# Two merge logit blocks of branch A as a pair of seven products, with filler dealt by need

## The chip, the cores and the metric

One NeuronCore of a Trainium2 chip runs the whole program. The metric is the device time of one execution in microseconds (us). TensorE (PE in the rows) does the matrix products, VectorE (DVE) and ScalarE (ACT) the elementwise work, GpSimd (POOL) some of it, and SyncE (SP) issues nearly all transfers (DMA) as one queue in order.

## What is computed

One encoder layer over 1024 frames and 1024 channels, in float32:

```
h = x @ w_in                     # split into q, k, v, gate_a, alpha_low, pool_in, gate_b, merge_logits
o = gla_chunked(q, k, v, logsigmoid(alpha_low @ w_alpha_up + b_alpha) / 16)    # 4 heads, chunks of 64 frames
y_a = rmsnorm(o) * gla_norm_g * silu(gate_a)                 # branch A, attention
y_b = pool(pool_in) * silu(gate_b)                           # branch B, trailing windows
g_a, g_b = split(sigmoid(merge_logits + b_merge))
y = (g_a * (y_a @ w_proj_a) + g_b * (y_b @ w_proj_b)) @ w_out
out = layernorm(2 ** 0.25 * x + y) * ln_g + ln_b
```

Inside a chunk of the attention every pair of frames (t, s) is weighted by exp(-|G_t - G_s|), in both directions of time; between chunks a state is carried.

## The kernel before, in words

Every float32 product is made of three products of a faster matrix type: each operand is split into a high part, rounded by ACT (`whi`, `xh`), and a rest made by DVE (`wlo`, `xl`), both by `split` at L52 and L53, and high*high, high*low and low*high add up in PSUM.

The program has two stages. The **attention stage** makes q, k and v and runs the four heads one after the other. A head (the loop `for h in range(H)`) builds scaled copies `qs` and `ks` at five distances (`level`), multiplies them (`scores`, into `ps_s`), and DVE merges each result into the tile `Pc` under a mask (L407). `place` copies `Pc` into the block-diagonal tile `P` (L410 on ACT, L411 on DVE). Then `outputs` multiplies `P` with v and `qi` with the carried states `st` (into `ps_o`, L441 and L443). `norm` scales the result, and in the next head `out_t` transposes it (L476) into a staging tile `oTs`, in two halves, whose four DMAs each (L478) store it in DRAM. `ends` prepares the next head: its tiles `e` (L311), `ke` and `cq`, and the decays. A head's own products on PE are small, with long chains on DVE between them, so `fill` puts other products in between, the **filler**: a generator gives one product at a time, with an assumed price (216 ns for 512 columns), and `fill(ns)` takes products until that much is paid. The filler is, in order: the q, k and gate projections of heads 1 to 3 (`q_gen`, `k_gen`, `z_gen`), the rest of v (`v1_gen`, 264 columns each), and the eight blocks of branch A's merge logits (`la_gen`), each 48 products of 512 columns. ACT copies a finished block's logits into the one tile of pool `sg`, and SP stores them (L296). What filler is left when the heads are done runs then.

In the **second stage** every 1024x1024 projection is cut in 2x2 parts and computed with seven part products in place of eight (class `Pair`: two blocks of 128 output channels, 7 x 12 = 84 products of 512 columns, where plain blocks need 2 x 48). The operands are combinations of parts of x (`xT`), y_b, y_a or w_o, made ahead. The pairs run in the order of the list `items`: pool input and its gate (`pi`, `gb`), gate of branch A (`gta`), merge logits of branch B (`lb`), the two projections (`pb`, `pa`), and then the output pairs `o` with the layer norm. `gate_a` loads the stored logits of branch A and applies the sigmoid.

A scheduler decides the order on each engine from the program's order, priorities (`tc.high_priority`) and a simulated timeline. After that every engine runs its own list strictly in that order, and waits where an input, or the buffer it writes, isn't ready. A tag of a pool has `bufs` buffers: tag `E`, with two, holds in turn the level tiles `e`, the tiles of `ends`, and `oTs`.

Of the kernel before, what the change touches and what calls it, by code (L numbers as in the profile page):

```python
# [7 lines left out]
F32 = mybir.dt.float32  # L8
# [3 lines left out]
AF = mybir.ActivationFunctionType  # L12
# [4 lines left out]
P = 128  # L17
S = 1024
D = 1024
KB = D // P  # L20
NT = S // P
H = 4
DV = 256
CH = 64
NPR = S // P
# [11 lines left out]
def encoder_layer(ctx: ExitStack, tc: tile.TileContext, xT, x, w_av, w_v, w_blk, w_up, b_al, g_norm,  # L37
                  w_pool, p_scale, b_mrg, w_pa, w_pb, w_o, ln_g, ln_b, ident_c, rcnt_c, masks_c, out):
    nc = tc.nc
    act, dve, pool_e, pe, sp = nc.scalar, nc.vector, nc.gpsimd, nc.tensor, nc.sync  # L40
# [40 lines left out]
    masks = const.tile([P, 5, CH], U8, name="masks")  # L81
# [4 lines left out]
    bm_t = const.tile([P, 16], F32, name="bm_t")  # L86
# [4 lines left out]
    gla = tc.alloc_tile_pool(name="gla", bufs=1)  # L91
# [51 lines left out]
                        yield n * 0.416 + 3  # L143

    def keep_v(tbs, outs, c0):
        for n, (tb, o) in enumerate(zip(tbs, outs)):
            dst = v[tb][:, c0:c0 + o.shape[1]]
            if n % 2:
                dve.tensor_copy(dst, o)  # L149
            else:  # L150
                act.copy(dst, o)

    accs = [ps_acc.tile([P, S], F32, tag="acc", name=f"ps_v0_{i}") for i in range(2)]
    scs = [ps_sc.tile([P, 512], F32, tag="sc", name=f"ps_v0_{i}") for i in (5, 6)]
# [95 lines left out]
    qt, kt_, gt = {}, {}, {}  # L250

    oT_d = dram.tile([H, 8, 32, 4, NPR, 32], F32, name="oT", tag="oT")
    la_d = [dram.tile([P, S], F32, name=f"la_{j}", tag=f"la_{j}") for j in range(KB)]
    pt = gla.tile([P, NPR, P], F32, name="P")
    pc = gla.tile([P, NPR, CH], F32, name="Pc")
# [5 lines left out]
    def z_gen(h):  # L261

        bias = b_al_t[:, h:h + 1]
        e = gla.tile([P, S], F32, tag="E", name=f"ze_{h}", bufs=2)
        m = gla.tile([P, S], F32, tag="qs", name=f"zm_{h}", bufs=2)
        for half in range(2):
            sl = slice(half * 512, half * 512 + 512)
            ps = ps_m.tile([P, 512], F32, tag="m", name=f"ps_z{h}_{half}")
            pe.matmul(ps, lhsT=up_w[:, h * P:h * P + P], rhs=a_rhs[:, sl], start=True, stop=True)
            act.activation(e[:, sl], ps, AF.Abs, bias=bias)  # L270
            dve.tensor_scalar(out=m[:, sl], in0=ps, scalar1=bias, scalar2=0.0, op0=ALU.add, op1=ALU.min)
            yield 216
        act.activation(e, e, AF.Exp, scale=-1.0)
        act.activation(e, e, AF.Ln, bias=1.0)
        dve.tensor_tensor(out=m, in0=m, in1=e, op=ALU.subtract)
        g = gla.tile([P, S], F32, tag="G", name=f"G_{h}", bufs=2)
        dve.tensor_tensor_scan(out=g, data0=smask, data1=m, initial=0.0, op0=ALU.mult, op1=ALU.add)
        gt[h] = g

    def q_gen(h):  # L280
        def then(ps):
            qt[h] = gla.tile([P, S], F32, tag="q", name=f"q_{h}", bufs=2)
            act.mul(qt[h], ps, QSCALE)
        return w_in_gen(h, f"q{h}", then)

    def k_gen(h):
        def then(ps):
            kt_[h] = gla.tile([P, S], F32, tag="k", name=f"k_{h}", bufs=2)
            dve.tensor_copy(kt_[h], ps)
        return w_in_gen(4 + h, f"k{h}", then)  # L290

    def la_gen(j, pool):
        def then(ps):
            s = pool.tile([P, S], F32, tag="sg", name=f"la_{j}")
            act.copy(s, ps)
            sp.dma_start(la_d[j], s)  # L296
        return w_in_gen(32 + j, f"la{j}", then)
# [97 lines left out]
    def scores(h, hl, li):  # L395

        qs, ks = gs[h][hl]
        ps = ps_sc.tile([P, 512], F32, tag="sc", name=f"ps_s{h}_{hl}")
        psv = ps.rearrange("p (b t) -> p b t", t=CH)
        for b in range(NPR):  # L400
            for c in range(2):
                cs = slice(b * P + c * CH, b * P + c * CH + CH)
                pe.matmul(psv[c * CH:c * CH + CH, b, :], lhsT=ks[:, cs], rhs=qs[:, cs], start=True, stop=True)  # L403
        if hl == 32:
            act.copy(pc, psv)
        else:
            dve.copy_predicated(out=pc, mask=masks[:, li - 1:li, :].to_broadcast([P, NPR, CH]), data=psv)  # L407

    def place(h):
        act.copy(pt[:CH, :, :CH], pc[:CH])  # L410
        dve.tensor_copy(pt[CH:, :, CH:], pc[CH:])  # L411

    def states(h):

        d, hs = gs[h], slice(h * DV, h * DV + DV)
        st = gla.tile([P, NPR - 1, DV], F32, tag="st", name=f"st_{h}", bufs=1)
        d["st"] = st
        for b0 in range(0, NPR - 1, 2):
            ps = (ps_m.tile([P, 512], F32, tag="m", name=f"ps_st{h}_{b0}") if b0 < 4 else
                  ps_sc.tile([P, 512], F32, tag="sc", name=f"ps_st{h}_{b0}"))  # L420
            bs = range(b0, min(b0 + 2, NPR - 1))
            for b in bs:
                pst = ps[:, (b - b0) * DV:(b - b0) * DV + DV]
                pe.matmul(pst, lhsT=d["ket"][:, b, :], rhs=v[b][:, hs], start=True, stop=True)
            with tc.high_priority(offset=100):
                for b in bs:
                    pst = ps[:, (b - b0) * DV:(b - b0) * DV + DV]
                    if b:
                        dve.scalar_tensor_tensor(out=st[:, b, :], in0=st[:, b - 1, :], scalar=d["dec"][:, b:b + 1],
                                                 in1=pst, op0=ALU.mult, op1=ALU.add)  # L430
                    else:
                        dve.tensor_copy(st[:, 0, :], pst)
# [38 lines left out]
    def out_t(h, half):  # L471

        hs = slice(h * DV, h * DV + DV)
        stage = gla.tile([P, 8, 4, 32], F32, tag="E", name=f"oTs_{h}_{half}", bufs=2)
        for b in range(4):
            dve.transpose(stage[:, :, b, :], v[half * 4 + b][:, hs].rearrange("p (j t) -> p j t", t=32))  # L476
        for i in range(4):
            sp.dma_start(oT_d[h, :, :, i, half * 4:half * 4 + 4, :].rearrange("j d b t -> d j (b t)"),  # L478
                         stage[32 * i:32 * i + 32].rearrange("d j b t -> d j (b t)"))


    def v1_gen(grp, tb0):
        acc = [ps_acc.tile([P, S], F32, tag="acc", name=f"ps_v1_{grp}_{tb0 + i}") for i in (0, 2)]
        tbs = range(tb0, tb0 + 4)
        outs = [acc[i // 2][:, i % 2 * 512:i % 2 * 512 + 264] for i in range(4)]
        yield from v_gen(w_v[grp], 264, f"v{grp}_{tb0}", tbs, outs)
        keep_v(tbs, outs, 496 + grp * 264)

    def chain(gens):
        for g in gens:  # L490
            yield from g

    owed = [0.0]

    def fill(ns):
        owed[0] += ns
        while owed[0] > 0:
            t = next(filler, None)
            if t is None:
                return  # L500
            owed[0] -= t

    sg = tc.alloc_tile_pool(name="sg", bufs=1, side="right")
    for g in (q_gen(0), z_gen(0), k_gen(0)):
        for _ in g:
            pass
    filler = chain([q_gen(1), z_gen(1), k_gen(1), v1_gen(0, 0), v1_gen(0, 4),
                    z_gen(2), q_gen(2), k_gen(2), v1_gen(1, 0), v1_gen(1, 4),
                    z_gen(3), q_gen(3), k_gen(3)] + [la_gen(j, sg) for j in range(8)])
    ends(0)  # L510
    starts(0)
    for h in range(H):
        todo = 42500
        steps = 12

        def f():
            fill(todo / steps)

        level(h, 32)
        if h == 0:  # L520
            fill(5000)
            todo -= 5000
        f()
        scores(h, 32, 0)
        cross_chunk(h)
        level(h, 16)
        f()
        k_transposed(h)
        single_frames(h)
        level(h, 8)  # L530
        f()
        scores(h, 16, 1)
        level(h, 4)
        f()
        scores(h, 8, 2)
        states(h)
        level(h, 2)
        if h:
            out_t(h - 1, 0)
        f()  # L540
        scores(h, 4, 3)
        if h:
            out_t(h - 1, 1)
        f()
        scores(h, 2, 4)
        place(h)
        f()
        if h + 1 < H:
            ends(h + 1)
        for b0 in range(0, NPR, 2):  # L550
            f()
            outputs(h, b0)
        if h + 1 < H:
            starts(h + 1)
        norm(h)
        f()
    for g in range(2):
        WO.ahead(g, lambda n, nm: gla.tile([P, 2, 512], F32, tag={"22": "KET", "12": "q", "11": "k", "21": "G"}[n], name=nm,
                                           bufs=1 if n == "22" else 2), dve)
    fill(10400)  # L560
    out_t(H - 1, 0)
    out_t(H - 1, 1)
    fill(1e9)
# [249 lines left out]
    for n, q in enumerate((0, 2, 1, 3)):  # L813
        items.append(gate_pair(f"gta{q}", 8 + 2 * q, AF.Silu, y_a(2 * q), hooks=more[n]))

    def keep(j0):
        def then(t):
            for i in range(2):
                sp.dma_start(gb_d[j0 + i], t(i))
        return then  # L820

    more = [ahead(YA, 0), ahead(YA, 1), None, change(X, YB)]
    for q in range(4):
        items.append(gate_pair(f"lb{q}", 40 + 2 * q, AF.Sigmoid, keep(2 * q), bias=8 + 2 * q, hooks=more[q]))


    m_last = {}
# [32 lines left out]

    def gate_a(t, j, cs):
        sp.dma_start(t, la_d[j][:, cs])
        act.activation(t, t, AF.Sigmoid, bias=bm_t[:, j:j + 1])

    for q in range(4):
        items.append(gated(f"pb{q}", 2 * q, YB, w_pb, lambda t, j, cs: sp.dma_start(t, gb_d[j][:, cs]), None,
# [188 lines left out]
```

## Time and profile before

| | us |
|---|---|
| median of 3 runs (972.33 to 977.69) | 973.58 |
| the profiled execution, its own time | 975.38 |
| its span, first to last instruction | 973.6 |
| PE busy in the span | 932.1 (96%) |
| DVE busy | 750.7 (77%) |
| ACT busy | 399.8 (41%) |
| POOL busy | 111.4 (11%) |

The profiled execution is one run; 1.8 us of its time lie outside its span. Busy shares are averages over both stages. A PE that is busy is not always at its peak, since overlapping products are all counted.

### The profile page before, as it was taken

The page shows a single profiled execution, that of the slowest core. Times are in us where ns is not written, and L with a number is a line of the kernel's source. Part 1 is how long each engine was busy: PE and PEld are TensorE (multiplying, and loading weights), DVE is VectorE, ACT ScalarE, POOL GpSimd, SP SyncE. Part 2 cuts the span into 40 slices and gives each one's busy share as a digit, 9 for nine tenths or more (in the row PEclk, how much of TensorE's full clock was granted, in tenths as well). Part 3 has the DMA queues.
Part 4 walks back from the last instruction along what each step waited for, and adds up shares of the span by engine and source line. Part 5 has one row for each costly group of instructions (what it writes and reads, how often), then busy time and mean ns, then how long its engine had stood idle before and what let it go on. Part 6 is the DMA issues. An engine that isn't in the chain of part 4 may idle for free. (4 is left out here: it accounts for less than half of the span.)

```text
span 973.6 us, 13056 instructions
## 1 busy us (share of the span) xinstructions
PE 932.1 (96%) x4744; PEld 755.8 (78%) x4744; DVE 750.7 (77%) x1144; ACT 399.8 (41%) x676; POOL 111.4 (11%) x59
## 2 busy tenths in 40 slices
PE   9999889899899999999999999999999999997995
PEld 6887887787677787788878788888888888775874
DVE  5459969859859655878696878788788887799787
ACT  5155335235142124433333333345562543544571
POOL 1523313313324000000000000000000000000022
PEclk9999999999999999999999999999999999997998
DMA  9931110330513738243212179799596787679254
GB/s 288 331 109 35 51 53 26 77 103 24 151 49 121 261 127 309 103 154 138 98 54 87 53 258 342 284 343 336 177 344 215 256 307 215 209 233 335 76 109 107
DMA packets 84144, 169.14 MB, mean 174 GB/s; under 512 B 11456, under 2 KB 28096, under 8 KB 84080
## 3 DMA queue, kind: packets, MB, share of 16 engines
q1 hardware_dynamic: 83216, 165.16, 49.7%
q0 software_dynamic: 864, 3.15, 1.9%
q8 instruction: 37, 0.61, 0.3%
q14 instruction: 27, 0.22, 0.1%
HBM read 114.80 MB, written 53.48 MB: 173 GB/s over the span
## 5 line engine op out<-in xcount | busy, mean ns | idle before, releaser
L455 POOL TENSOR_TENSOR rsr_ln<-rsa_ln,mhalf 128x2 f32<-128x2 f32 (+1 forms) x5 | 5.1, 1014 | 583.0 <-PE psc_o L634 571.0
L392 POOL TENSOR_TENSOR ks<-k,e 128x1024 f32<-128x1024 f32 x20 | 57.8, 2900 | 77.3 <-ACT e L388 63.1
L123 PE MATMUL ps_la<-xh,whi_la 128*128 128x512 f32 x128 | 51.3, 401 | 0.0
L123 PE MATMUL ps_la<-xh,wlo_la 128*128 128x512 f32 x128 | 51.1, 399 | 0.0
L123 PE MATMUL ps_la<-xl,whi_la 128*128 128x512 f32 x128 | 51.0, 398 | 0.0
L141 PE MATMUL ps_v<-whi_v,xh 128*128 128x264 f32 x128 | 38.4, 300 | 3.6 <-DVE v L149 3.1
L388 ACT ACTIVATE e<-e 128x1024 f32<-128x1024 f32 x20 | 21.1, 1059 | 42.8 <-DVE e L387 39.6
L141 PE MATMUL ps_v<-whi_v,xl 128*128 128x264 f32 x128 | 38.6, 302 | 0.0
L141 PE MATMUL ps_v<-wlo_v,xh 128*128 128x264 f32 x128 | 38.0, 301 | 0.0
L52 ACT CAST whi_gb<-raw_gb 128x512 fp32r<-128x512 f32 x28 | 17.3, 621 | 49.0 <-PE psd_pi L634 14.8
L391 DVE TENSOR_TENSOR qs<-q,e 128x1024 f32<-128x1024 f32 x20 | 33.5, 1674 | 2.1 <-ACT e L388 2.0
L52 ACT CAST whi_lb<-raw_lb 128x512 fp32r<-128x512 f32 x28 | 17.4, 621 | 37.1 <-PE psd_lb L634 9.3
L52 ACT CAST whi_gta<-raw_gta 128x512 fp32r<-128x512 f32 x28 | 17.3, 618 | 33.9 <-PE psd_gta L634 10.1
L52 ACT CAST whi_pi<-raw_pi 128x512 fp32r<-128x512 f32 x28 | 17.4, 620 | 32.6 <-PE psd_gb L634 7.0
L52 ACT CAST whi_pb<-raw_pb 128x512 fp32r<-128x512 f32 x28 | 17.1, 619 | 32.8 <-PE psd_pb L634 11.2
L446 DVE COPY v<-ps_o 128x256 f32<-128x256 f32 x32 | 13.3, 421 | 21.8 <-PE ps_o L443 15.8
L141 PEld LDWEIGHTS ps_v<-whi_v,xh 128*128 128x128 f32 x128 | 25.3, 198 | 4.5 <-DVE v L149 3.4
L123 PEld LDWEIGHTS ps_la<-xh,whi_la 128*128 128x128 f32 x128 | 24.1, 188 | 5.7 <-issue 0.4
L123 PEld LDWEIGHTS ps_la<-xh,wlo_la 128*128 128x128 f32 x128 | 24.1, 188 | 5.4
L403 PEld LDWEIGHTS ps_s<-qs,ks 128*64 128x64 f32 x640 | 20.8, 138 | 9.5 <-issue 9.3
L123 PEld LDWEIGHTS ps_la<-xl,whi_la 128*128 128x128 f32 x128 | 24.1, 188 | 5.3
L52 ACT CAST whi_o<-raw_o 128x512 fp32r<-128x512 f32 x28 | 16.9, 617 | 25.1 <-DVE raw_o L619 8.8
(586 smaller groups left out, 3066.4 us busy)
## 6 DMA issues: line engine op xcount, KB each, us to landing
raw_v<-in_w_v SPq DMA_DIRECT2D x16, 264.0 KB, 2.6
xp<-in_xT SPq DMA_DIRECT2D x8, 512.0 KB, 6.8
oT<-oTs SPq DMA_DIRECT2D x32, 128.0 KB, 2.6
raw_la<-in_w_blk SPq DMA_DIRECT2D x8, 512.0 KB, 3.5
wop<-in_w_o SPq DMA_DIRECT2D x8, 512.0 KB, 4.3
la<-la SPq DMA_DIRECT2D x8, 512.0 KB, 3.6
raw_pi<-in_w_blk SPq DMA_DIRECT2D x16, 256.0 KB, 3.8
raw_gb<-in_w_blk SPq DMA_DIRECT2D x16, 256.0 KB, 2.6
```

What stands on the lines that cost most here:

```text
L52: act.copy(hi, src)
L123: pe.matmul(ps[:, half * 512:half * 512 + 512], lhsT=a, rhs=mov(b, k, half), start=(i == 0), stop=(i == 23))
L141: pe.matmul(o, lhsT=sta(a, k, tb), rhs=w(k - k0)[b], start=(k == 0 and i == 0), stop=(k == KB - 1 and i == 2))
L388: act.activation(e, e, AF.Exp, scale=1.0 / TAU)
L391: dve.tensor_tensor(out=qs, in0=qt[h], in1=e, op=ALU.mult)
L392: pool_e.tensor_tensor(out=ks, in0=kt_[h], in1=e, op=ALU.mult)
L403: pe.matmul(psv[c * CH:c * CH + CH, b, :], lhsT=ks[:, cs], rhs=qs[:, cs], start=True, stop=True)
L446: dve.tensor_copy(v[b][:, hs], po)
L455: pool_e.tensor_tensor(out=r, in0=a, in1=mhalf[:, :w], op=ALU.pow)
```

## The change

It does six things. (1) `NLA = 6`: only six of branch A's eight logit blocks stay in the filler; blocks 6 and 7 become a `gate_pair` named `la6`, which stands in `items` between the last `gta` and the first `lb`, and stores finished gates, so that `gate_a` leaves out the sigmoid for them. (2) `todo`, the filler dealt per head, goes from 42500 to 38500 ns, and the portion ahead of the last head's transposes from 10400 to 18000. (3) `until` takes filler until a named point of it is passed: head h's v before `states(h)`, the next head's k before `ends(h + 1)`. (4) The copies in `keep_v`, `scores` and `place` get a priority raised by 100. (5) `out_t` stages heads 0 to 2 in the one tile of pool `sg` and no longer in tag `E`; the last head stays in `E`. (6) `keep` takes the tensor it stores to.

```diff
@@ keep_v, the copies of scores, and place
+        with tc.high_priority(offset=100):
@@ out_t
-        stage = gla.tile([P, 8, 4, 32], F32, tag="E", name=f"oTs_{h}_{half}", bufs=2)
+        pool, tag = (sg, "sg") if h < H - 1 else (gla, "E")
+        stage = pool.tile([P, 8, 4, 32], F32, tag=tag, name=f"oTs_{h}_{half}", bufs=1 if h < H - 1 else 2)
@@ filler
+    passed = set()
+    def mark(nm):
+        passed.add(nm)
+        yield 0
+    def until(nm):
+        while nm not in passed:
+            owed[0] -= next(filler)
...
-    filler = chain([q_gen(1), z_gen(1), k_gen(1), v1_gen(0, 0), v1_gen(0, 4),
-                    z_gen(2), q_gen(2), k_gen(2), v1_gen(1, 0), v1_gen(1, 4),
-                    z_gen(3), q_gen(3), k_gen(3)] + [la_gen(j, sg) for j in range(8)])
+    filler = chain([q_gen(1), z_gen(1), k_gen(1), mark("k1"), v1_gen(0, 0), v1_gen(0, 4), mark("v1"),
+                    z_gen(2), q_gen(2), k_gen(2), mark("k2"), v1_gen(1, 0), v1_gen(1, 4), mark("v2"),
+                    z_gen(3), q_gen(3), k_gen(3), mark("k3")] + [la_gen(j, sg) for j in range(NLA)])
...
-        todo = 42500
+        todo = 38500
...
+        if 0 < h < 3:
+            until(f"v{h}")
         states(h)
...
         if h + 1 < H:
+            until(f"k{h + 1}")
             ends(h + 1)
...
-    fill(10400)
+    fill(18000)
     out_t(H - 1, 0)
@@ second stage
+    for j in range(NLA, KB, 2):
+        items.append(gate_pair(f"la{j}", 32 + j, AF.Sigmoid, keep(la_d, j), bias=j,
+                               hooks=ahead(WO, (j - NLA) // 2) if NLA < 6 else None))
...
     def gate_a(t, j, cs):
         sp.dma_start(t, la_d[j][:, cs])
-        act.activation(t, t, AF.Sigmoid, bias=bm_t[:, j:j + 1])
+        if j < NLA:
+            act.activation(t, t, AF.Sigmoid, bias=bm_t[:, j:j + 1])
```

Lines of the changed kernel are a few numbers higher than before. The orders below name a tile with its buffer number, and the line first.

The first place is DVE's list in head 2, from the merge of the second-last scores (`ps_s_4`) to the half of `place` that DVE does. Before:

```order
L407 COPY_PREDICATED Pc<-masks,ps_s_4_2269 128x512
L322 TENSOR_TENSOR cq_2371<-q_2173,e_3_2362 128x512
L325 TENSOR_TENSOR cq_2371<-q_2173,k_2335 128x8x32 x2
L327 TENSOR_TENSOR cq_2371<-q_2173,e_3_2368 128x16
L329 TENSOR_TENSOR cq_2371<-q_2173,k_2335 128x16
L407 COPY_PREDICATED Pc<-masks,ps_s_2_2313 128x512
L328 TENSOR_TENSOR cq_2371<-cq_2371,k_2335 128x16
L330 TENSOR_TENSOR cq_2371<-q_2173,ke_2372 128x16
L386 TENSOR_TENSOR e_32_2535<-G_2022 128x16x32
L387 TENSOR_TENSOR e_32_2535<-G_2022 128x16x32
L411 COPY P<-Pc 64x8x64
```

And the same stretch of DVE's list in the changed kernel:

```order
L410 COPY_PREDICATED Pc<-masks,ps_s_4_2212 128x512
L324 TENSOR_TENSOR cq_2346<-q_2274,e_3_2337 128x512
L329 TENSOR_TENSOR cq_2346<-q_2274,e_3_2343 128x16
L410 COPY_PREDICATED Pc<-masks,ps_s_2_2254 128x512
L415 COPY P<-Pc 64x8x64
```

The next head's products with k and its first level tile `e_32`, which stood ahead of the copy into `P`, stand behind it now. In heads 0 and 1 they stay ahead of it.

The second place is DVE's list in head 1, with the transposes of head 0's outputs (`oTs_0` and `oTs_1`, the two halves) and the tile `e` of `ends`. Before:

```order
L476 STREAM_TRANSPOSE oTs_1_1624<-v_107 128x8x32
L429 SCALAR_TENSOR_TENSOR st_1554<-st_1554,dec_1082,ps_st_4_1565 128x256
L307 COPY egl_1718<-e_2_1716 128x16
L53 TENSOR_TENSOR wlo_v_0_4_0_1756<-raw_v_0_4_1753,whi_v_0_4_0_1755 128x528
L309 TENSOR_TENSOR dec_1720<-egl_1718 128x8
L429 SCALAR_TENSOR_TENSOR st_1554<-st_1554,dec_1082,ps_st_6_1570 128x256
L289 COPY k_1670<-ps_k_1520 128x1024
L53 TENSOR_TENSOR wlo_v_0_6_0_1795<-raw_v_0_6_1792,whi_v_0_6_0_1794 128x528
L311 TENSOR_TENSOR e_2_1722<-G_1357 128x1024
L407 COPY_PREDICATED Pc<-masks,ps_s_4_1606 128x512
```

And in the changed kernel, from the last transpose of the first half to the first of the second:

```order
L481 STREAM_TRANSPOSE oTs_0_1543<-v_103 128x8x32
L53 TENSOR_TENSOR wlo_v_0_2_0_1735<-raw_v_0_2_1732,whi_v_0_2_0_1734 128x528
L436 COPY st_1516<-ps_st_0_1517 128x256
L313 TENSOR_TENSOR e_2_1678<-G_1394 128x1024
L311 TENSOR_TENSOR dec_1676<-egl_1674 128x8
L433 SCALAR_TENSOR_TENSOR st_1516<-st_1516,dec_1055,ps_st_0_1517 128x256
L433 SCALAR_TENSOR_TENSOR st_1516<-st_1516,dec_1055,ps_st_2_1522 128x256 x2
L481 STREAM_TRANSPOSE oTs_1_1598<-v_104 128x8x32
```

The tile `e` of `ends` is written between the two halves' transposes now and no longer behind both; five other instructions stand between the halves as well.

The third place is SP's list in head 3: the stores of head 2's two halves (`oTs_0` and `oTs_1`), the loads `wop` of w_o, and the stores of logit blocks, whose tile in `sg` the changed kernel shares with `oTs`. Before:

```order
L296 DMA la_518<-la_2669 128x1024
L216 DMA wop_1_3082<-in_w_o 128x2x512
L478 DMA oT<-oTs_0_2772 32x8x128 x4
L216 DMA wop_1_3078<-in_w_o 128x2x512
L216 DMA wop_1_3080<-in_w_o 128x2x512
L478 DMA oT<-oTs_1_2815 32x8x128 x4
L216 DMA wop_0_3056<-in_w_o 128x2x512
```

And in the changed kernel:

```order
L298 DMA la_517<-la_2633 128x1024
L217 DMA wop_1_2976<-in_w_o 128x2x512
L217 DMA wop_1_2978<-in_w_o 128x2x512
L483 DMA oT<-oTs_0_2696 32x8x128 x4
L217 DMA wop_0_2954<-in_w_o 128x2x512
L483 DMA oT<-oTs_1_2738 32x8x128 x4
```

Two loads into the buffers of tags `q` and `k`, which stood between the two halves' stores, stand ahead of both now.

## Rows read from the trace of the kernel before

**Rows 1.** The page: busy us, share of the span and instructions of each engine.

```profile
PE 932.1 (96%) x4744; PEld 755.8 (78%) x4744; DVE 750.7 (77%) x1144; ACT 399.8 (41%) x676; POOL 111.4 (11%) x59
```

**Rows 2.** Stretches: from:to, length, busy us by engine, granted clock, DMA.

```profile
85.00:129.00 44.00, 38.30 (x354) 33.05 (x353) 40.46 (x55) 21.36 (x29) 15.10 (x6) 0.95 0.18 55
129.00:196.00 67.00, 61.94 (x484) 53.37 (x483) 54.16 (x85) 25.53 (x46) 18.90 (x7) 0.98 0.18 47
196.00:270.00 74.00, 68.96 (x499) 57.81 (x500) 56.93 (x98) 29.04 (x52) 19.29 (x7) 0.98 0.30 92
...
640.00:740.00 100.00, 100.00 (x433) 81.04 (x432) 80.90 (x109) 51.65 (x74) 0.00 (x0) 1.00 0.83 300
```

**Rows 3.** Who PE waited for from 60 to 340 us: total us, times, longest.

```profile
PE ps_o L441 <- ACT P L410: 4.0, 1, 4.0
PE ps_o L441 <- DVE P L411: 3.4, 2, 2.7
PE ps_v L141 <- DVE v L149: 3.1, 1, 3.1
PE ps_s L403 <- DVE egl L307: 2.6, 2, 1.3
PE ps_st L424 <- DVE Pc L407: 2.2, 2, 1.6
PE ps_v L141 <- DVE k L289: 0.5, 1, 0.5
PE ps_s L403 <- DVE Pc L364: 0.5, 1, 0.5
```

**Rows 4.** PE in order of time: filler, first outputs of heads, first pair.

```profile
132.61 0.28 PE L141 MATMUL ps_v<-whi_v,xl 128*128 128x264 f32 x1
132.73 1.02 PE L441 MATMUL ps_o<-v,P 128*128 128x256 f32 x4
...
196.25 2.08 PE L441 MATMUL ps_o<-v,P 128*128 128x256 f32 x4 [4.02 <-ACT P L410]
...
269.67 1.10 PE L441 MATMUL ps_o<-v,P 128*128 128x256 f32 x4 [2.71 <-DVE P L411]
...
333.40 1.10 PE L441 MATMUL ps_o<-v,P 128*128 128x256 f32 x4 [0.69 <-DVE P L411]
...
375.79 0.39 PE L634 MATMUL psa_pi<-xh,whi_pi 128*128 128x512 f32 x1
```

**Rows 5.** DVE in order of time, heads 0 to 2: start, us, idle before.

```profile
128.53 0.42 DVE L411 COPY P<-Pc 64x512 f32<-64x512 f32 x1
...
189.54 1.23 DVE L311 TENSOR_TENSOR e<-G 128x1024 f32<-128x1024 f32 x1 [3.48 <-DMA oT<-oTs]
...
260.42 1.23 DVE L311 TENSOR_TENSOR e<-G 128x1024 f32<-128x1024 f32 x1 [2.72 <-DMA oT<-oTs]
261.57 1.22 DVE L289 COPY k<-ps_k 128x1024 f32<-128x1024 f32 x1
...
268.39 0.68 DVE L387 TENSOR_TENSOR e<-G 128x512 f32<-128x512 f32 x1
```

**Rows 6.** The stores of oTs: issue ns (min/median/max), and time to landing.

```profile
L478 SPq DMA_DIRECT2D oT<-oTs x32: 302/463/1479, 177.4 to 365.0; - x32
...
DMA to landing us min/median/max: 2.1/2.6/4.7
```

**Rows 7.** ACT at the seam: the first pair's first weight.

```profile
370.35 0.62 ACT L52 CAST whi_pi<-raw_pi 128x512 fp32r<-128x512 f32 x1 [4.49 <-DMA raw_pi<-in_w_blk]
```

**Rows 8.** SP's queue at the seam.

```profile
377.32 0.33 SPq L296 DMA_DIRECT2D la<-la  x1
377.69 0.43 SPq L209 DMA_DIRECT2D xT<-xT_0d  x1
```

**Rows 9.** DVE: the eight multiplies of norm, in head 1 and head 3.

```profile
150.91 5.40 DVE L469 SCALAR_TENSOR_TENSOR v<-v,rsr_o,gn 128x256 f32<-128x256 f32 x8
...
355.99 3.26 DVE L469 SCALAR_TENSOR_TENSOR v<-v,rsr_o,gn 128x256 f32<-128x256 f32 x8
```

More of the change, by code (lines that the diff above doesn't have):

```diff
@@ L145, in keep_v @@
     def keep_v(tbs, outs, c0):
[L146 to L151, printed above, removed]
+        with tc.high_priority(offset=100):
+            for n, (tb, o) in enumerate(zip(tbs, outs)):
+                dst = v[tb][:, c0:c0 + o.shape[1]]
+                if n % 2:
+                    dve.tensor_copy(dst, o)
+                else:
+                    act.copy(dst, o)
     accs = [ps_acc.tile([P, S], F32, tag="acc", name=f"ps_v0_{i}") for i in range(2)]
@@ L252, in encoder_layer @@
     oT_d = dram.tile([H, 8, 32, 4, NPR, 32], F32, name="oT", tag="oT")
+    NLA = 6
     la_d = [dram.tile([P, S], F32, name=f"la_{j}", tag=f"la_{j}") for j in range(KB)]
@@ L403, in scores @@
                 pe.matmul(psv[c * CH:c * CH + CH, b, :], lhsT=ks[:, cs], rhs=qs[:, cs], start=True, stop=True)
[L404 to L407, printed above, removed]
+        with tc.high_priority(offset=100):
+            if hl == 32:
+                act.copy(pc, psv)
+            else:
+                dve.copy_predicated(out=pc, mask=masks[:, li - 1:li, :].to_broadcast([P, NPR, CH]), data=psv)
     def place(h):
-        act.copy(pt[:CH, :, :CH], pc[:CH])
-        dve.tensor_copy(pt[CH:, :, CH:], pc[CH:])
+        with tc.high_priority(offset=100):
+            act.copy(pt[:CH, :, :CH], pc[:CH])
+            dve.tensor_copy(pt[CH:, :, CH:], pc[CH:])
     def states(h):
@@ L814, in encoder_layer, with keep @@
         items.append(gate_pair(f"gta{q}", 8 + 2 * q, AF.Silu, y_a(2 * q), hooks=more[n]))
-    def keep(j0):
+    def keep(d, j0):
         def then(t):
             for i in range(2):
-                sp.dma_start(gb_d[j0 + i], t(i))
+                sp.dma_start(d[j0 + i], t(i))
         return then
+    for j in range(NLA, KB, 2):
+        items.append(gate_pair(f"la{j}", 32 + j, AF.Sigmoid, keep(la_d, j), bias=j,
+                               hooks=ahead(WO, (j - NLA) // 2) if NLA < 6 else None))
     more = [ahead(YA, 0), ahead(YA, 1), None, change(X, YB)]
     for q in range(4):
-        items.append(gate_pair(f"lb{q}", 40 + 2 * q, AF.Sigmoid, keep(2 * q), bias=8 + 2 * q, hooks=more[q]))
+        items.append(gate_pair(f"lb{q}", 40 + 2 * q, AF.Sigmoid, keep(gb_d, 2 * q), bias=8 + 2 * q, hooks=more[q]))
     m_last = {}
```

## The prediction

> **What bounds the kernel now.** I read the page first. PE is busy 96% of the span, DVE 77% [rows 1], so the question is where PE loses time and whether DVE stands behind it. The view by stretches gives both. In the second stage (640 to 740 us) PE is busy all the time with 433 products in 100 us, that is 0.231 us for a product of 512 columns; DVE is busy 81% [rows 2]. Each product put there or taken away counts in full. In the attention stage DVE is busy 40.5 of the 44 us of head 0 and 54.2 and 56.9 us of the 67 and 74 us that follow [rows 2]. There PE waits: the view of PE's waits adds up to 16.3 us, for DVE or for what DVE releases, and the largest (4.0 and 3.4) are first products with `P` that wait for `place` [rows 3]. The granted clock of these three stretches is 0.95, 0.98 and 0.98 [rows 2], which is 2.2, 1.3 and 1.5 us of full clock lost: stretches at the lower of TensorE's two levels (1.2 GHz, against 2.4) behind the waits.
>
> PE's list in order of time shows the heads: the first output product starts at 132.73, 196.25, 269.67 and 333.40 us, and the first pair at 375.79 [rows 4]. The intervals are 63.5, 73.4, 63.7 and 42.4 us, and PE waits in the first three for 5.3 (4.0 and 1.3), 4.6 (2.7, 1.3 and 0.6) and 0.7 us, in head 0 for the other 5.7 [rows 3, 4].
>
> Two causes can be read from DVE's list. In heads 1 and 2 the tile `e` at L311 stood 3.48 and 2.72 us at the head of DVE's queue until a store of `oTs` had read its buffer of tag `E`, and the merges of the scores and `place` stood behind it [rows 5]. And in head 2 the order puts k's copy (1.22 us), the products with k and `e_32` (two of 0.68) ahead of the copy into `P` [rows 5].
>
> **The arithmetic.** Two logit blocks fewer are 2 x 48 = 96 products, 96 x 0.231 = 22.2 us; a pair more is 84 products, 19.4 us. Net 2.8 us off. The pair's conversions (7 high parts on ACT, 7 rests and 10 sums on DVE) lie beside PE in a stage where DVE has 19 us in 100 free [rows 2]; if that cover failed, PE would wait for DVE there, which it does nowhere between 640 and 740.
>
> The Trainium skill ("TensorE: Matmul & The Clock Gate", section "Wait — 56ns, not 53.3ns?") gives 215.7 ns from one product of 512 columns to the next at full clock. The rows show 231, 7% more, at a clock of 1.00; by the page's figure the two numbers would be 20.7 and 18.1 us, net 2.6, and nothing else in the sum would change.
>
> **The waits, head by head.** What an interval takes is the longer of PE's own work and DVE's. From the order I counted the filler in each interval. A product of v's 264 columns takes 0.12 us [rows 4].
>
> *Up to head 0's first output.* DVE works nearly without a gap, and its list up to the copy into `P` holds the same work as before. That copy ended at 128.95 [rows 5], but PE came only at 132.73, because it had waited itself (for v's PSUM buffer, which `keep_v` frees late, and for merges) and had run at the lower clock. With these copies raised PE comes in time: first output at 129, DVE's bound. In that time it does 28 v products more and one of 512 columns less, 3.2 us. Bounds: 126 (DVE's few gaps go) to 132.7 (as now).
>
> *Head 0 to head 1.* Filler: the same 96 products of 512 columns, 100 v products in place of 131, so 3.8 us less. PE's own work is 63.5 - 5.3 - 3.8 = 54.4 us. DVE has 54.2 us of work [rows 2], plus the next head's `e_32` (1.4 us), which comes ahead of `P` now, plus waits that stay: some 2 us at PE's pace during the outputs, and a new one. The staging tile has one buffer now, so the second half's transposes wait for the first half's four stores: 4 x 0.46 us of issue and 2.6 of landing [rows 6], 4.5 us, of which `e`, written between the halves now, covers 1.2 [rows 5], and six short instructions some more: a wait of 0.5 to 3.3. I take 2. Behind those transposes at DVE's head stand the merges and `place`, and PE waits for these. Sum 59.6 us: DVE sets this interval, PE idles 5 us in it as before, and the first output starts at 188.6. Bounds 55 to 64.
>
> *Head 1 to head 2.* 102 products in place of 132, and 134 v products for 131: 6.6 us less. PE's own: 73.4 - 4.6 - 6.6 = 62.2, with 1.5 us of clock loss left in. DVE: 56.9 less `e_32` done earlier and what goes behind `P` (1.22 + 1.4 + small ones), about 52, and 4 of waits. PE sets it; with 1.3 us for waits that no order excludes, 63.5: next first output at 252.1. Bounds 60.7 (no wait, no clock loss) to 67.
>
> *Head 2 to head 3.* 166 products for 193: 6.2 us less. 63.7 - 0.7 - 6.2 = 56.8, and 1.5 us for the shared tile, since the logit stores use it too: 58.3, next at 310.4. Bounds 56.8 to 62.
>
> *Head 3 to the first pair.* 116 products for 155: 9.0 us less, 42.4 - 9.0 = 33.4. The cover shrinks: 84 products (19.4 us) follow the last output product in place of 107 (24.7), 5.3 us less. The first pair's first weight is converted at 370.35 to 370.97 [rows 7], 4.8 us ahead of need, and its loads follow the last head's outputs, so it comes 0.5 us late; the next weights perhaps another 0.5. The loads of `xT` stand in SP's queue right behind the last logit store [rows 8], before and after, so they shift with the end of the filler and cost nothing new. I take 1 us: first pair at 344.8. Bounds 0 to 5.3, all of the lost cover.
>
> Before, the first pair came at 375.8, so 31.0 us are gained; the added pair takes 19.4: net 11.6. That is 2.8 of arithmetic and 8.8 of the 21.3 us that waits and clock cost, with the seam's 1 us taken off. The sigmoids that `gate_a` leaves out, the marks of `until` and the rest of the second stage I cost at nothing: the list of the output pairs, where the kernel ends, is nearly unchanged. The profiled execution took 975.4; 975.4 - 11.6 = 963.8. The median of the runs is 1.8 below that execution, so I predict **962**.
>
> **The rivals.** *All waits go.* If DVE keeps pace between heads 0 and 1 too (54.4 in place of 59.6) and the small allowances (1.3, 1.5, 1.0 and 1.5 of clock) vanish, 10.5 more: 951.5. For it: DVE's waits for stores are gone from tag `E`. Against it: 54.2 us of DVE work alone already fills that interval.
>
> *The waits change places.* Less filler means that PE reaches each dependency sooner, and DVE's work does not shrink. If DVE, at 52 us of work with gaps like today's 13 (67 less 54.2), sets the interval after head 1 as well, that costs some 3 us, the interval after head 2 another 2 or 3, and the seam 3: about 971. The Trainium skill ("Perfetto Trace Analysis", section "Optimizing Scalar/DVE Operations") speaks for it: GpSimd and DVE share a port for reading SBUF. The trace agrees so far: the eight multiplies of `norm` took 5.40 us in head 1, and 3.26 in head 3 [rows 9]; GpSimd worked 18.9 us in the first of these stretches [rows 2]. In a shorter interval GpSimd's work lies denser.
>
> *Slower, through the single staging tile.* In head 3 the first half's stores stand in SP's list behind two loads of w_o that need buffers of `q` and `k`, free only when the last level is built; the second half's transposes stand at DVE's head ahead of both last merges and `place`. In head 1 they also do. If the transposes wait 7 to 8 us there and not 0.5 to 3.3, in each of three heads, 16.5 us are lost against the forecast and the kernel passes 978.5. For it speaks that a store in tag `E` already held DVE 3.48 us [rows 5]; against it that in head 2 eleven other instructions stand between the halves.
>
> **Chances.** Forecast, 957 to 968.7: 0.53. All waits gone, below 957: 0.17. Changed places, 968.7 to 978.5: 0.21. Slower, above: 0.09. A measurement of this kernel tells about 0.5% from no change, 4.9 us either way of 973.6. So: faster 0.70, same 0.21, slower 0.09. The range is 953 to 974: it reaches into the first two rivals and leaves out the slow one.
>
> **What would show it.** First output products at about 129, 189, 252 and 310, and the first pair at 345 us. No wait of L313 for a store of `oTs`, but one of the transposes, up to 3.3 us, in heads 1 and 3. PE's largest wait is that for `P` in head 1, about 5 us; in head 2 hardly any. The pair `la6` takes 19 to 20 us. Wrong would make it: a wait of more than 5 us at the transposes, a second long wait for `P`, or a seam where PE waits for the first weights or `xT` by more than 3 us.

## The result, and the profile after

The changed kernel takes 969.14 us (median of 13 runs, 966.51 to 971.98) against 975.12 for the kernel before, run with it (13 runs); the ratio is 0.9931, 95% interval [0.9913, 0.995], that is 4.9 to 8.5 us less. Forecast were 962 us and 11.6 us less. The sign and the range held; the size is about half, and the profiles show that it came about in another way than forecast.

The page of the changed kernel, busy us by engine (it answers to [rows 1]): PE is busy 6.6 us less, and DVE 14 us more in a shorter span.

```profile
PE 925.5 (96%) x4732; PEld 753.1 (78%) x4732; DVE 765.0 (79%) x1156; ACT 400.7 (42%) x680; POOL 110.0 (11%) x59
```

PE's list in order of time, the first output product of each head, the first pair, and the first products of the pair `la6` and of the one after it (answers to [rows 4]):

```profile
129.94 0.59 PE L445 MATMUL ps_o<-v,P 128*128 128x256 f32 x2
...
190.79 0.45 PE L445 MATMUL ps_o<-v,P 128*128 128x256 f32 x1 [0.72 <-DVE P L415]
...
255.42 0.38 PE L445 MATMUL ps_o<-v,P 128*128 128x256 f32 x1
...
316.10 0.48 PE L445 MATMUL ps_o<-v,P 128*128 128x256 f32 x1
...
354.61 0.50 PE L651 MATMUL psa_pi<-xh,whi_pi 128*128 128x512 f32 x1
...
611.19 0.40 PE L651 MATMUL psa_la<-xh,whi_la 128*128 128x512 f32 x1
...
630.52 0.39 PE L651 MATMUL psa_lb<-xh,whi_lb 128*128 128x512 f32 x1
```

The first pair comes 21.2 us earlier (forecast 31.0), and `la6` takes 19.33 us (forecast 19.4). From the first pair to the end of the span it was 973.6 - 375.8 = 597.8 us and is 965.4 - 354.6 = 610.8: 13.0 us more and not 19.4. So two errors of opposite sign stand in the sum. The stretches between those starts (columns as in [rows 2]):

```profile
85.00:129.94 44.94, 41.88 (x402) 37.03 (x402) 41.55 (x56) 21.40 (x29) 12.14 (x6) 1.00 0.20 61
129.94:190.79 60.85, 55.91 (x433) 47.25 (x431) 55.95 (x88) 25.95 (x47) 20.67 (x7) 0.97 0.18 47
190.79:255.42 64.63, 61.67 (x470) 52.80 (x471) 54.35 (x86) 27.70 (x50) 16.30 (x6) 0.97 0.32 97
255.42:316.10 60.68, 57.30 (x399) 45.74 (x397) 50.01 (x79) 17.81 (x35) 18.44 (x7) 1.00 0.35 114
316.10:354.61 38.51, 35.33 (x146) 28.42 (x146) 16.74 (x37) 7.52 (x22) 1.64 (x1) 0.96 0.55 178
```

And who PE waited for from 60 to 360 us (answers to [rows 3]):

```profile
PE ps_st L428 <- DVE Pc L410: 6.0, 4, 2.1
PE ps_o L445 <- ACT ps_o L451: 5.1, 3, 3.1
PE ps_q L123 <- DVE v L150: 1.9, 1, 1.9
PE ps_s L405 <- DVE st L433: 1.4, 1, 1.4
PE ps_s L405 <- DVE qs L393: 1.2, 1, 1.2
PE ps_s L405 <- DVE Pc L366: 1.1, 1, 1.1
PE ps_o L445 <- DVE P L415: 0.7, 1, 0.7
```

These add up to 17.4 us, where 16.3 stood before [rows 3], and the granted clock of the five stretches costs 1.8 + 1.9 + 1.5, about 5.3 us, where it was 5.0. The 7.4 us of waits for `P` have become 0.7, and others have come: 6.0 for the merges of the scores and 5.1 for the outputs' PSUM buffers. In sum nothing of waits and clock was recovered; the 21.2 us are about the price of the 96 products of the two blocks, 22.2.

The largest single wait, 3.1 us, stands in head 3. DVE's list there:

```profile
320.38 5.07 DVE L198 TENSOR_TENSOR wop<-wop,wop 128x1024 f32<-128x1024 f32 x4 [3.80 <-DMA wop<-in_w_o]
325.38 0.42 DVE L450 COPY v<-ps_o 128x256 f32<-128x256 f32 x1
326.37 0.76 DVE L450 COPY v<-ps_o 128x256 f32<-128x256 f32 x2 [0.57 <-ACT ps_o L451]
327.76 0.42 DVE L450 COPY v<-ps_o 128x256 f32<-128x256 f32 x1 [0.64 <-ACT ps_o L451]
```

and PE's, a few us later:

```profile
327.39 1.22 PE L445 MATMUL ps_o<-v,P 128*128 128x256 f32 x2 [3.12 <-ACT ps_o L451]
```

The four sums of w_o's second group (L198) stood at DVE's head for 3.80 us, until a load had landed, and worked for 5.07 us. The copies of the outputs (L450) stood behind them; the squares on ACT wait for the copies, and PE's third output for the squares. The load was that of a tile in `KET`, which the first group must have left:

```profile
314.45 0.38 SPq L217 DMA_DIRECT2D wop<-in_w_o  x1
```

The two products after the wait took 1.22 us, about twice the 0.59 of the first output row above, and the granted clock is 0.96 in this stretch and 0.50 from 327 to 329 us: the wait brought a piece at the lower of the two levels with it.

### The profile page after: what moved, and what is told of

It is laid out like the page before. It is cut to its first block, busy times and chain, and to the rows that moved or that the text cites. A ratio compares the mean times of both kernels' runs of the same rounds, so it can differ in the third digit from the quotient of the medians.

```text
span 965.4 us, 13072 instructions
## 1 busy us (share of the span) xinstructions
PE 925.5 (96%) x4732; PEld 753.1 (78%) x4732; DVE 765.0 (79%) x1156; ACT 400.7 (42%) x680; POOL 110.0 (11%) x59
## 5 line engine op out<-in xcount | busy, mean ns | idle before, releaser
L394 POOL TENSOR_TENSOR ks<-k,e 128x1024 f32<-128x1024 f32 x20 | 55.4, 2771 | 96.5 <-ACT e L390 47.0
L390 ACT ACTIVATE e<-e 128x1024 f32<-128x1024 f32 x20 | 21.2, 1059 | 57.2 <-DVE e L389 57.2
L123 PE MATMUL ps_la<-xl,whi_la 128*128 128x512 f32 x96 | 38.8, 404 | 0.0
L123 PE MATMUL ps_la<-xh,whi_la 128*128 128x512 f32 x96 | 38.3, 399 | 0.0
L123 PE MATMUL ps_la<-xh,wlo_la 128*128 128x512 f32 x96 | 38.3, 399 | 0.0
L52 ACT CAST whi_pi<-raw_pi 128x512 fp32r<-128x512 f32 x28 | 17.4, 620 | 37.7 <-DMA raw_pi<-in_w_blk 9.5
L393 DVE TENSOR_TENSOR qs<-q,e 128x1024 f32<-128x1024 f32 x20 | 30.9, 1543 | 2.3 <-ACT e L390 1.6
L52 ACT CAST whi_lb<-raw_lb 128x512 fp32r<-128x512 f32 x28 | 17.4, 621 | 36.6 <-PE psd_lb L651 8.5
L123 PE MATMUL ps_q<-xh,whi_q 128*128 128x512 f32 x64 | 25.8, 404 | 2.0 <-DVE v L150 1.9
L53 DVE TENSOR_TENSOR wlo_pi<-raw_pi,whi_pi 128x512 fp32r<-128x512 f32 x28 | 19.2, 686 | 10.5 <-ACT whi_pi L52 10.5
L405 PE MATMUL ps_s<-qs,ks 128*64 128x64 f32 x640 | 23.6, 225 | 3.7 <-DVE st L433 1.4
L123 PE MATMUL ps_k<-xh,whi_k 128*128 128x512 f32 x64 | 26.6, 416 | 0.0
L123 PE MATMUL ps_k<-xh,wlo_k 128*128 128x512 f32 x64 | 26.2, 409 | 0.0
```

Source lines behind the costliest of these rows:

```text
L52: act.copy(hi, src)
L53: (lo_eng or dve).tensor_tensor(out=lo, in0=src, in1=hi.bitcast(F32), op=ALU.subtract)
L123: pe.matmul(ps[:, half * 512:half * 512 + 512], lhsT=a, rhs=mov(b, k, half), start=(i == 0), stop=(i == 23))
L390: act.activation(e, e, AF.Exp, scale=1.0 / TAU)
L393: dve.tensor_tensor(out=qs, in0=qt[h], in1=e, op=ALU.mult)
L394: pool_e.tensor_tensor(out=ks, in0=kt_[h], in1=e, op=ALU.mult)
```

## The experiments

Times are medians, ratios are to the kernel before on the same chip. "The changed kernel" is 969.14 us, 0.9931.

| run | edit | us | ratio, 95% interval |
|---|---|---|---|
| e1 | all edits but the pair | 977.25 | 1.0012 [0.9994, 1.003] |
| e2 | the pair alone | 990.94 | 1.0141 [1.0121, 1.0161] |
| e3 | second group's sums on GpSimd | 964.62 | 0.9873 [0.9857, 0.989] |
| e4 | staging back in tag E | 968.5 | 0.9906 [0.9887, 0.9925] |
| e5 | output copies on ScalarE | 957.23 | 0.9803 [0.9783, 0.9822] |
| e6 | no raised copies | 967.88 | 0.9917 [0.9896, 0.9937] |
| e7 | old filler numbers | 983.9 | 1.0078 [1.0058, 1.0099] |
| e8 | e3 and e4 | 966.42 | 0.9892 [0.9872, 0.9912] |
| e9 | fixed turn of weight buffers, as in the changed kernel | 980.75 | 1.005 [1.003, 1.007] |
| e10 | fixed turn, as in the kernel before | 982.25 | 1.0073 [1.0049, 1.0096] |
| e11 | e3 and e5 | 957.9 | 0.9815 [0.979, 0.9839] |
| e12 | the kernel before, output copies on ScalarE | 976.53 | 1.0008 [0.9988, 1.0028] |

The theory after the result: **the gain in the attention is the products taken away; the waits only changed places.** The rival is the forecast's own: the dealing, the raised copies and the staging recover waits by themselves.

**e1, the dealing without the pair**

```diff
-    NLA = 6
+    NLA = 8
```

> All eight logit blocks stay in the filler and no pair is added; every other edit of the change is kept. If the gain of the change is arithmetic and the waits only change places (my theory), this is the kernel before within its noise: 972 to 977 us, PE waits between 60 us and the first pair still 14 to 18 us. If the dealing by need, the raised copies and the staging recover waits of their own, as the forecast had it (8.8 us), it is 964 to 968 us with waits under 10.

No difference to before. Its waits from 60 us to the first pair add up to 20.8 us, more than my 14 to 18, and the first pair comes at 376.39 (before 375.79). With the new numbers, the dealing, the raised copies and the staging together recover nothing; at these numbers the rival falls (e7 shows another side of it).

**e2, the pair without the dealing**

```diff
 (kernel before)
-    ... [la_gen(j, sg) for j in range(8)])
+    ... [la_gen(j, sg) for j in range(6)])
+    for j in range(6, KB, 2):
+        items.append(gate_pair(f"la{j}", 32 + j, AF.Sigmoid, keep(la_d, j), bias=j, ...))
```

> The kernel before with blocks 6 and 7 moved into a pair and nothing else changed (42500 ns of filler per head, 10400 at the end, no raised copies, staging in tag E). My theory: the filler is dealt out too early, so that few products stand between the last output and the first pair; PE then waits 10 to 18 us for the first weights, and the kernel takes 983 to 992 us; the change's other edits are what makes the pair pay. Rival, the move of the blocks alone brings the gain and the other edits nothing: 967 to 971 us.

As expected: 13.9 us slower than before. PE's waits from 60 to 370 us, the first three rows:

```profile
PE psa_pi L635 <- ACT whi_pi L52: 15.0, 1, 15.0
PE ps_o L442 <- ACT P L411: 4.0, 1, 4.0
PE ps_o L442 <- DVE P L412: 3.4, 2, 2.7
```

The order up to head 3 is that of before, so the missing 96 products are missing at the end, where they covered the last head's norm, its transposes, its stores and the first loads of weights.

**e3, the sums of w_o's second group on GpSimd**

```diff
-    WO.ahead(g, ..., dve)
+    WO.ahead(g, ..., (dve, pool_e)[g])
```

> The changed kernel with the four sums of w_o's second group on GpSimd in place of DVE. In the changed kernel these four stand at DVE's head in head 3, wait 3.8 us for a load and hold the copies of the outputs, and PE waits 3.1 us for those at half the clock afterwards. My theory: that wait goes, the interval from head 3's first output to the first pair shrinks from 38.5 to 34 to 35 us, 964 to 966 us in all. Rival, the end of the attention hangs on the chain of norm, stores and first loads anyway: the first pair comes as late as now, 968 to 970 us.

The last stretch of this kernel, from head 3's first output to the first pair:

```profile
315.01:348.42 33.41, 33.41 (x147) 27.59 (x147) 13.06 (x33) 7.77 (x21) 11.86 (x5) 1.00 0.62 204
```

38.51 has become 33.41, PE is busy for all of it, and the clock is 1.00. The theory holds: 5.1 us of this stretch hung on those sums. GpSimd took 10.45 us for the four, where DVE takes 5.07, and nothing waited for it. Of the 5.1 us, PE's wait is 3.1; most of the rest goes with the clock. e10 (below) has the same sums on DVE and the same wait (3.2 us), but a clock of 1.00, and its last stretch takes 36.89:

```profile
314.38:351.27 36.89, 33.70 (x147) 27.41 (x147) 16.72 (x37) 7.51 (x21) 1.64 (x1) 1.00 0.54 180
```


**e4, the staging of the transposes back in tag E**

```diff
-        pool, tag = (sg, "sg") if h < H - 1 else (gla, "E")
-        stage = pool.tile(..., tag=tag, bufs=1 if h < H - 1 else 2)
+        stage = gla.tile(..., tag="E", bufs=2)
```

> The changed kernel with the transposes of heads 0 to 2 staged in the two buffers of tag E again, everything else kept. If the separate staging is worth what the forecast gave it (waits of 3.5 and 2.7 us of e for a store gone from DVE's head, 2 given back at the transposes): 972 to 975 us. If the waits only change places (my theory): within 1.5 us of the changed kernel, 968 to 971 us, with e waiting for stores again and the transposes and the logit copy no longer.

The waits for the stores of `oTs` in this kernel, from 60 to 352 us; L313 writes the tile `e` of `ends` that DVE makes, L306 the other one, which ACT makes:

```profile
DVE oTs L480 <- DMA oT<-oTs: 1.4, 1, 1.4
DVE e L313 <- DMA oT<-oTs: 0.6, 2, 0.3
ACT e L306 <- DMA oT<-oTs: 17.4, 2, 12.6
```

On DVE the waits of `e` [rows 5] do not come back with the old staging (0.6 us). They come back on ACT, whose `e` takes over the buffers that the stores hold; before and in the changed kernel ACT's list shows no wait for these stores at this tile. So it is not the separate tile that freed DVE's head. The pair is not it either, since in e2 DVE's `e` still waits 6.2 us. Of the numbers, `until` and the raised copies no run shows which does it. With the separate tile the transposes wait 4.0 us (two waits, the longest 2.7), and ACT's copy of a logit block 3.6 us for a store. The intervals of the two ratios overlap, so the separate staging is worth nothing that can be told.

**e5, the output copies on ScalarE**

```diff
-            dve.tensor_copy(v[b][:, hs], po)
+            act.copy(v[b][:, hs], po)
```

> The changed kernel with the copies of the output blocks (32 of 0.42 us) on ScalarE in place of DVE. My theory: DVE's work sets the interval from head 0's to head 1's first output (60.8 us in three kernels, whatever PE did in it), so with 3.4 us less of it that interval shrinks to 57 to 58.5; and the sums of w_o at DVE's head in head 3 hold no copy any more, so the last interval is 34 to 35: 960 to 963 us. Rival, not DVE's amount of work but the chain of the merges sets the first interval (or ScalarE delays its own exponentials): it stays at 60 to 61, and only the last interval shrinks: 964 to 966 us.

The best of the twelve: 1.97% below before. Its stretches:

```profile
85.00:130.06 45.06, 41.96 (x403) 37.11 (x401) 41.66 (x56) 21.40 (x29) 12.28 (x6) 1.00 0.20 61
130.06:190.00 59.94, 55.93 (x429) 46.79 (x427) 52.78 (x80) 28.35 (x55) 17.83 (x7) 0.97 0.19 48
190.00:252.82 62.82, 61.94 (x482) 53.39 (x481) 51.65 (x79) 30.45 (x58) 17.75 (x7) 1.00 0.33 100
252.82:308.28 55.46, 55.46 (x394) 45.08 (x392) 42.89 (x69) 20.83 (x43) 17.17 (x7) 1.00 0.36 117
308.28:341.59 33.31, 33.31 (x148) 27.45 (x146) 14.06 (x29) 10.69 (x30) 1.64 (x1) 1.00 0.67 220
```

The total is below what I expected, but the gain does not stand where I expected it. Between heads 0 and 1 DVE has 3.2 us less work and the interval shrinks by 0.9 only: the amount of DVE's work does not set that interval, and this part of my theory fell. PE still waits 4.0 us there, 2.7 of it in one wait for a merge. The gain stands in the interval after head 2 (60.68 to 55.46) and in the last (38.51 to 33.31); in both PE no longer waits at all. Of the 5.2 us after head 2, some 1.4 are six filler products that lie in the interval before it now.

**e6, without the raised copies** (the three `with tc.high_priority(offset=100):` of the change left out)

> The changed kernel without the three raised priorities (the copies into v, of the scores and into P). Few instructions change their place (one copy of v's, two merges on DVE, some ten products on PE). My theory: no difference, 967 to 971 us, first output of head 0 within 1 us of 129.9. If the forecast's reason for that first output (the raised copies bring PE there in time) holds, it comes at 131.5 to 133 and the kernel takes 971 to 973.

No difference that can be told, and head 0's first output comes at 129.72. The forecast's reason for it, the raised copies, falls. What comes with the early output is shown under e7 and e12.

**e7, the old numbers**

```diff
-        todo = 38500
+        todo = 42500
...
-    fill(18000)
+    fill(10400)
```

> The changed kernel with the numbers of before: 42500 ns of filler per head and 10400 ahead of the last transposes. My theory: the numbers are what keeps products for the end of the attention; with the old ones PE waits 10 to 15 us for the first weights of the second stage, 980 to 988 us. Rival, the heads wait less with more filler in each and the end has cover enough: 967 to 972 us.

PE's waits from 60 to 365 us, the first three:

```profile
PE psa_pi L651 <- ACT whi_pi L52: 15.7, 1, 15.7
PE ps_st L428 <- DVE Pc L410: 4.2, 4, 1.8
PE ps_v L141 <- DVE v L150: 3.2, 1, 3.2
```

The wait for the first weights, 15.7 us where I expected 10 to 15, is the one of e2. But e7 is faster than e2, 1.0078 against 1.0141, some 6 us, and both have the pair and the old numbers: here the other edits (`until`, the raised copies, the staging) do recover waits. PE's waits other than that for the weights add up to 11.2 us, and to 16.2 in e2, and those for `P`, 7.4 us in e2, are 1.1. With the new numbers this gain is gone (e1). No run has these edits with the old numbers and without the pair, so what they are worth alone stays open.

Head 0's first output comes at 132.88, as before, with the copies raised; in the ten kernels with 38500 it comes at 129.6 to 130.9, raised or not. The stretch up to it:

```profile
85.00:132.88 47.88, 41.95 (x377) 36.75 (x376) 44.71 (x57) 22.02 (x29) 17.65 (x7) 0.93 0.19 57
```

The clock is 0.93 in it, as before and in e2, and 1.00 in all ten kernels with 38500. e12 shows that the share of filler is not needed for that.

**e8, e3 and e4 together**

> The second group's sums of w_o on GpSimd and the staging back in tag E, the rest as changed. The first alone gave 964.6, the second alone 968.5 against about 969. If the two work in different places (last interval; heads 1 to 3), they add up: 962 to 964 us, last interval 33.5 to 34.5. If tag E gained only because it let the sums of w_o come earlier, it adds nothing: 964 to 966 us.

They do not add up. The last interval is 34.2 us, and the 966.42 lie just above the second reading. That tag E gained by letting the sums come earlier fits e4's own last interval (34.79, against 38.51), and is not shown beyond that.

**e9 and e10, the turn of the weight buffers**

The high and low parts of each split weight go into four buffers each. In the compiled programs these are taken in another turn (order) in the second stage of the kernel before than in the changed one. Both experiments fix the turn:

```diff
 (changed kernel)
-        hi = ring.tile(..., tag="whi")
-        lo = ring.tile(..., tag="wlo")
+        k = turn[0] % 4; turn[0] += 1
+        hi = ring.tile(..., tag=f"whi{W[k]}", bufs=1)
+        lo = ring.tile(..., tag=f"wlo{L[k]}", bufs=1)
 e9:  W = 1,3,0,2   L = 2,3,0,1
 e10: W = 3,2,1,0   L = 2,3,1,0
```

> The changed kernel with the four buffers each of the split weights (high and low part) taken in a fixed turn, the turn that the changed kernel's second stage has. From 550 us on, a product started every 0.2303 us in the changed kernel and five of its variants, and every 0.2320 us in the kernel before and three others, at a granted clock of 1.00 in all ten. My theory: where the parts of the weights lie decides it; here 0.2303 again. The total depends on the attention too, whose turn is also fixed now: 965 to 975 us. Rival, the places do not matter: the pace is the same here and in the next run, whichever it is.

> As the run above, each engine's instructions in the same order, with the turn of the slower four kernels: the high parts in the other order of buffers, the low parts with two of four exchanged. Theory: 0.2320 us per product from 550 us on, and 2.5 to 3 us more than the run above in all (1700 products by 0.0017). Rival: no difference above 1 us.

Busy time and products of PE in the same 100 us of the second stage, first in the kernel before:

```profile
650.00:750.00 100.00, 100.00 (x433) 81.04 (x432) 78.91 (x109) 49.44 (x72) 0.00 (x0) 1.00 0.80 284
```

in the changed kernel:

```profile
650.00:750.00 100.00, 100.00 (x436) 81.61 (x435) 80.37 (x113) 48.65 (x72) 0.00 (x0) 1.00 0.77 269
```

in e9:

```profile
650.00:750.00 100.00, 100.00 (x436) 81.61 (x435) 77.66 (x106) 50.05 (x73) 0.00 (x0) 1.00 0.80 283
```

and in e10:

```profile
650.00:750.00 100.00, 100.00 (x433) 81.02 (x432) 77.39 (x107) 49.81 (x74) 0.00 (x0) 1.00 0.81 278
```

436 products with the one turn and 433 with the other, the same instructions in the same order, at a granted clock of 1.00: the place of the weights' parts decides the pace, and it followed the turn in the two new kernels as it had in the ten profiles before. Whether the turn of the high parts or that of the low parts does it, these two runs can't tell, since both change. The four `lb` pairs show it too: from first to last start of their 336 products 77.70 us before, 77.14 changed, 77.14 in e9 and 77.71 in e10. The total follows less clearly: 1.5 us between the medians, with intervals that overlap, where I expected 2.5 to 3. Both miss the 965 to 975 us that I expected of e9: by their ratios they are some 12 and 14 us slower than the changed kernel. The loss stands in the second stage, which takes 625.8 us in e9 and 610.8 in the changed kernel; PE's waits there add up to 18.0 us in e9, where they were 10.5, and the largest new ones are for the tiles `gb` (5.9).

**e11, e3 and e5 together**

> The output copies on ScalarE and the second group's sums of w_o on GpSimd, the rest as changed. The copies alone gave 957.2 and left no wait behind head 2's outputs. If the sums held nothing but those copies: 955.5 to 958.5, no gain. If taking 5 us more from DVE in head 3 still helps, or GpSimd slows DVE: outside of that, to either side.

No gain over e5: the sums held nothing but those copies.

**e12, the kernel before with the output copies on ScalarE**

> The kernel before with one edit, the copies of the output blocks on ScalarE in place of DVE. In the changed kernel that edit took 12 us off. Before, PE waits for 4.6 us in the intervals after heads 1 and 2 (4.0 and 0.6 us) that 3.4 us less of DVE's work per head could shorten, and the two intervals after that hold 2.7 and 0.7. My theory: the edit pays mainly because the changed kernel's shorter filler has put PE within reach of DVE's work; here it brings 2 to 5 us, 971 to 974. Rival, DVE's load alone is what it relieves, in either kernel alike: 963 to 967 us.

No gain; my 2 to 5 us were too much as well. The edit that takes 12 us off the changed kernel is worth nothing that can be told in the kernel before. PE's waits there still add up to 16.4 us, and the largest are again other ones (from 60 to 378 us):

```profile
PE ps_o L441 <- DVE P L411: 4.2, 2, 3.1
PE ps_v L141 <- DVE k L289: 4.0, 2, 3.5
PE ps_v L141 <- DVE v L149: 3.2, 1, 3.2
```

The stretch up to head 0's first output answers the question that e7 left:

```profile
85.00:129.66 44.66, 38.72 (x375) 33.60 (x374) 42.16 (x57) 22.02 (x29) 16.17 (x7) 1.00 0.20 57
```

This kernel has the old numbers and no raised copies, and up to that product PE, DVE and ACT have the lists of the kernel before. PE waits 6.0 us from 60 to 132 us, where it waited 5.7. Yet the output comes at 129.66 and not at 132.73: the clock is 1.00 in this execution and 0.93 in the other. So what comes with the early output is a clock that doesn't fall. Why it fell in some executions and not in others, and whether the smaller share of filler helps, no run shows.

## Why the prediction was half right

**The arithmetic** held: 96 products left the attention, and `la6` took 19.33 us for 19.4, without a wait for its conversions.

**The waits** are the step that failed: "that is 2.8 of arithmetic and 8.8 of the 21.3 us that waits and clock cost". Nothing of the 21.3 was recovered; 22.7 stand there after. By interval:

| | forecast | changed | e3 | e5 |
|---|---|---|---|---|
| first output of head 0 | 129 | 129.94 | 130.29 | 130.06 |
| head 0 to 1 | 59.6 | 60.85 | 60.82 | 59.94 |
| head 1 to 2 | 63.5 | 64.63 | 63.05 | 62.82 |
| head 2 to 3 | 58.3 | 60.68 | 60.85 | 55.46 |
| head 3 to first pair | 34.4 | 38.51 | 33.41 | 33.31 |
| first pair at | 344.8 | 354.61 | 348.42 | 341.59 |

The first three terms are 0.9 to 1.3 us too short. For head 1 to 2 the miss goes with the clock, which was 0.97 in that stretch: e1 and e3 have the changed kernel's lists up to there, and at a clock of 1.00 the same interval took 63.05 in both. The last is the largest miss, 4.1 us. I looked for the lost cover at the first weights and `xT`, and gave it 1 us; it was lost at the outputs, because I did not look at what stands at the head of DVE's queue there: the four sums of w_o, one of them behind a load. Before, DVE waited for such a load too, but only two sums stood between it and the first copies:

```profile
336.60 2.48 DVE L197 TENSOR_TENSOR wop<-wop,wop 128x1024 f32<-128x1024 f32 x2 [3.35 <-DMA wop<-in_w_o]
```
e3 gives the term back: 33.41, where I had 33.4 for PE's own work. The term after head 2 was 2.4 short: PE waits 3.3 us there, twice for the merges ahead of the states products and once for another copy of a score. e5 removes these, so DVE's copies of the outputs have a part in them too.

The interval in which I let DVE set the time, head 0 to 1, was right to 1.3 us, but for a reason that e5 does not bear out: with 3.2 us less of DVE's work it stayed at 59.94. PE has slack there: with its clock at 0.97 (changed) and at 1.00 (e1, e3) the interval is 60.8. Which chain sets it stays open. Head 0's first output came at 129.94 for 129, but not through the raised copies (e6).

**The signs.** `e` waits for no store, and the transposes wait 1.3 us in head 1 and 2.7 in head 3, as said. The largest wait is not that for `P` in head 1 (0.7 us); in that interval PE waits 2.1 us for a merge, 1.2 for `qs` and 0.9 for an output buffer instead. At the seam PE waits for neither weights nor `xT`.

**The rest of the second stage**, costed at nothing, brought 6.3 us: 13.0 more in place of 19.3. From about 550 us on a product starts every 0.2303 us in place of 0.2320: some 1,600 products that both kernels have, by 0.0017, 2.7 us. PE's waits from the first pair on fall from 12.4 to 10.5, 1.9 us: those of the pairs `gb` (1.0) and of the pool's products (`ps_mx`, 0.9) are gone. What removed them stays open, and the other 1.7 us I can't assign. So perhaps 2.7 of the measured 4.9 to 8.5 us come from where buffers happen to lie. Without the 6.3 us, the 21.2 gained in the attention less the 19.3 of the pair would have left 1.9 of the forecast 11.6: that the gain came to half of the forecast is luck.

**The rivals.** In the attention it went as in the second rival, the waits changed places; with the 6.3 us of the second stage, which I had not forecast, the time came out just below that rival's 971. With 969.14 us it lies at the lower edge of the band that the chances gave that rival (968.7 to 978.5), and not in the forecast's own. The eight multiplies of the second `norm`, which took 3.26 us at 226.72 before, take 5.39 now, since a `ks` of GpSimd's has come to lie on them (below). By the Trainium skill ("Perfetto Trace Analysis", section "Optimizing Scalar/DVE Operations") the two engines share a port for reading SBUF; the trace agrees, with those 2.1 us. The slow rival's place was right (transposes wait for the single tile, 1.3 and 2.7 us), its price of 7 to 8 us was not.

## What to carry to other kernels

When work leaves a filler, what is left must be dealt out anew: the pair costs 13.9 us with the old numbers (6.9 with the change's other edits, e7) and brings 6.0 with those edits and the new numbers. A shorter filler does not shorten the chains that it hid, so read, for each queue that PE will now reach sooner, what stands at its head and what that waits for, and not the sum of its work. And try again what once brought nothing: the output copies on ScalarE are worth 12 us after the change and none before it. Before giving an edit the credit for a shorter stretch, read the granted clock of that stretch: one and the same list of products took 44.7 and 47.7 us up to head 0's first output, at 1.00 and 0.93.

## What the hardware showed that I had not expected

Products of 512 columns started every 0.2303 or 0.2320 us at the same granted clock, depending on which SBUF buffers held the split weights; e9 and e10 differ in nothing else. Why one turn of the buffers is slower no run here shows.

A DVE instruction can take as long as the GpSimd instruction beside it. Three rows of the changed kernel; first the group of the second `norm`'s multiplies in DVE's list:

```profile
214.23 5.39 DVE L473 SCALAR_TENSOR_TENSOR v<-v,rsr_o,gn 128x256 f32<-128x256 f32 x8
```

in GpSimd's list:

```profile
216.68 2.66 POOL L394 TENSOR_TENSOR ks<-k,e 128x1024 f32<-128x1024 f32 x1 [3.29 <-PE ps_kt L376]
```

and in the view of the tile `v`, the shortest, median and longest of all 32 multiplies of the four heads in ns:

```profile
L473 DVE SCALAR_TENSOR_TENSOR v<-v,rsr_o,gn x32: 471/479/2632, 166.0 to 342.7; 128x256 f32<-128x256 f32 x32
```

In the group shown seven multiplies take their 0.48 us; the last starts at 217.0 and takes 2.61, about as long as `ks` on GpSimd, which starts 0.3 us before it. The groups of the first and third head have a `ks` beside them and such a multiply too (2.63 and 2.61 us). In the last head no GpSimd work lies beside the eight; the longest takes 0.49 us and the group 3.26, as before [rows 9].
